# Second product of an expert placed between the halves of the next expert's first product

## The chip, the cores and the metric

The kernel runs on one core of a Trainium2 chip. Times are device microseconds (us) of one execution of the whole program. TensorE (PE in the profile; PEld is its weight load) multiplies, VectorE (DVE) and ScalarE (ACT) work element by element, GpSimd (POOL) builds selections and issues indirect DMAs, SyncE (SP) issues the other DMAs. On-chip memory is SBUF; products gather in PSUM.

## The reference

One layer of a backbone: a token mixer, then a mixture of experts with 32 experts, of which every token goes to 4. The change is in the experts:

```python
def expert_block(args):
    xb, e = args
    hb = xb @ w1[e] + b1[e]
    x_glu = jnp.minimum(hb[:, ::2], SWIGLU_LIMIT)
    x_lin = jnp.clip(hb[:, 1::2], -SWIGLU_LIMIT, SWIGLU_LIMIT)
    act = x_glu * jax.nn.sigmoid(SWIGLU_ALPHA * x_glu) * (x_lin + 1)
    return act @ w2[e] + b2[e]
...
contrib = out[dest].astype(jnp.float32) * sorted_gate[:, None]
return jax.ops.segment_sum(contrib, sorted_tok, num_segments=n_tok).astype(h.dtype)
```

There are 1024 tokens of width 1024. `w1[e]` is 1024 x 2048 and `w2[e]` 1024 x 1024, in float32: 12 MiB of weights for each expert, 384 MiB in all, each read once.

## The kernel before

After the mixer (some 560 us; the routing overlaps the first experts) `experts` (line 1232) runs over 32 places `r`. The experts are sorted by load, and the places alternate a large and a small one: `CAPS[r]` is 122, 122, 126, 122, 132, 120 and so on to 176, 78, 182, 66 token columns.

An expert's weights come as 12 blocks of 1 MiB (`block`, line 1438): blocks 0 to 3 are the first half (1024 columns) of `w1`, 4 to 7 the second half, 8 to 11 are `w2`. They lie in ten buffers `raw`. SP issues the loads in the order of use, each as soon as a buffer is free (`loads`, line 1256). VectorE derives a low part of each block (`lower`, line 1446; buffers `lo`), because a product is made of three float16 or bfloat16 products. Lowering runs `AHEAD` = 4 blocks ahead of TensorE.

TensorE works in 12 units for each expert. A unit (`product`, line 1454) has 48 matmuls and uses two blocks: first-product units are (q, s) with quarter q of 0 to 3 and half s of the inner dimension; the second product has q of 4 and 5 in the order (4,0), (5,0), (4,1), (5,1). In all three parts of an expert the first two of its four blocks are used by s = 0 and the last two by s = 1. When a quarter of the first product is complete, `swiglu` (line 1487) turns it into a quarter of `act` in three stages, one in each of the following units; stages two and three need VectorE after ScalarE. A second-product unit with s = 0 reads quarters 0 and 1 of `act`, one with s = 1 quarters 2 and 3.

The schedule is a hand-written order in the loop at line 1388: `u` counts units, `t = u % 12` is the unit of the expert. In each unit are issued, in this order: the matmuls, the loads that became possible, the second halves of earlier transposes (`rest`), the lowering of block `u + 4`, one stage of each waiting swiglu or output step (`pend`), and then side work: transposes of the rows gathered for the next expert (`turn`, line 1326, from t = 7), transposes of the finished output rows of the expert before (`finish`, line 1343, from t = 1) whose rest scales the rows by their gate and adds them into DRAM by an indirect DMA on POOL (`acc`), the slots' index work for two experts (`batch`, line 1283, t = 5), the selection matrix of a later expert on POOL (`select`, line 1270, t = 0), and the indirect gather of a later expert's rows on POOL (`gather`, line 1321, t = 11). At t = 8 all swiglu stages that are left are issued at once, since the third unit of the second product (t = 10) needs them. Each scatter into `acc` waits on POOL for the landing of the one before. Every engine takes its own instructions in the order in which they were issued.

Of the kernel before, what the change touches and what calls it, by code (L numbers as in the profile page):

```python
# [12 lines left out]
F16 = mybir.dt.float16  # L13
# [11 lines left out]
NE = 32  # L25
# [28 lines left out]
CAPS = [BY_LOAD[q] for q in ORDER]  # L54
# [57 lines left out]
class K:  # L112
# [73 lines left out]
    def mixing(self, p1, up, sm, pm, pt, po):  # L186
# [767 lines left out]

        def channels(ct, U, V):
            pa = bank()
# [275 lines left out]
    def experts(self, routing):  # L1232

        nc, T = self.nc, self.T

        STEPS = [(q, s) for q in range(4) for s in range(2)] + [(4, 0), (5, 0), (4, 1), (5, 1)]
        U = [(r, q, s) for r in range(NE) for q, s in STEPS]
        used = lambda u: [u - u % 12 + 4 * (U[u][1] // 2) + 2 * U[u][2] + i for i in range(2)]  # L1240
        last = {v: u for u in range(len(U)) for v in used(u)}
        raw, low, info, B, X, A, Y, pss = {}, {}, {}, {}, {}, {}, {}, {}
        reg = {}
# [1 line left out]
        freed = set()  # L1245

        def load(u):
            r, b = u // 12, u % 12
            if b == 0:
                reg[r] = nc.sync.value_load(self.eid[0:1, r:r + 1], min_val=0, max_val=NE - 1)  # L1250
                B[r] = self.es_.tile([128, 24], F32, name="bias", bufs=3)
            raw[u] = self.block(reg[r], b // 4, b % 4)
            if b == 0:
                nc.sync.dma_start(B[r], self.biasd[:, bass.ds(reg[r], 1), :].rearrange("p a j -> p (a j)"))

        def loads(spare=0):
# [13 lines left out]
        def select(r, engine=nc.gpsimd, sel=None):  # L1270
            w = width(r)
            if sel is None:
                sel = self.ep.tile([128, NT, CMAX], BF, name="sel", bufs=3)
            if engine is nc.gpsimd:
                for t in range(NT):
                    engine.tensor_scalar(sel[:, t, 0:w], self.places[:, 0:w], self.prk[:, t, r:r + 1], None, op0=OP.is_equal)  # L1276
            else:
                nc.vector.tensor_tensor(sel[:, :, 0:w], self.places[:, None, 0:w].to_broadcast([128, NT, w]), self.prk[:, :, r:r + 1].to_broadcast([128, NT, w]), op=OP.is_equal)
            if CAPS[r] < ROWS[r]:
                engine.memset(sel[:, :, CAPS[r]:ROWS[r]], 0.0)  # L1280
            return sel
# [39 lines left out]
        def gather(r, name="rows"):  # L1321
            for b, (m, idx, gate) in enumerate(info[r]):
                rows[r, b] = self.ep.tile([128, D], F32, name=name, bufs=2)
                nc.gpsimd.indirect_dma_start(out=rows[r, b][0:m, :], out_offset=None, in_=self.Hd, in_offset=bass.IndirectOffsetOnAxis(ap=idx[0:m, :], axis=0))  # L1324

        def turn(r):

            if r >= NE:
                return []
            n = CAPS[r]  # L1330
            X[r] = self.ep.tile([128, 8, 3, n], F16, name="xT", bufs=2)
            out = []
            for b in range((n + 127) // 128):
                m = min(128, n - b * 128)
                parted = [(0, 4), (4, 8)] if m > 64 else [(0, 8)]
                out += [lambda b=b, m=m, ks=ks: self.turn(rows[r, b], X[r], ks, b, m) for ks in parted]
            return out

        def run(q):
            while q:  # L1340
                q.pop(0)()

        def finish(r):

            if r < 0:
                return []
            out = {}

            def step(b, m, idx, gate, h):
                if h == 0:  # L1350
                    out[b] = self.ep.tile([128, D], F32, name="orow", bufs=2)
                ps = self.px.tile([128, 4, 128], F32, name="px")
                for k in range(4):
                    nc.tensor.transpose(ps[0:m, k, :], Y[r][:, 4 * h + k, b * 128:b * 128 + m], self.ident)  # L1354

                def rest():
                    nc.scalar.activation(out[b][0:m, h * 512:(h + 1) * 512], ps[0:m].rearrange("p a n -> p (a n)"), AF.Copy, scale=gate[0:m, :])  # L1357
                    if h:
                        nc.gpsimd.indirect_dma_start(out=self.acc, out_offset=bass.IndirectOffsetOnAxis(ap=idx[0:m, :], axis=0), in_=out[b][0:m, :], in_offset=None, compute_op=OP.add)  # L1359

                return rest

            return [lambda b=b, m=m, idx=idx, gate=gate, h=h: step(b, m, idx, gate, h) for b, (m, idx, gate) in enumerate(info[r]) for h in range(2)]

        sels = {}
# [20 lines left out]

        pend, side, rest = [], [], []
        for u, (r, q, s) in enumerate(U):
            n, t = CAPS[r], u % 12
            bias = lambda j, r=r: B[r][:, j:j + 1]  # L1390
            if t == 0:
                A[r] = self.ep.tile([128, 8, 3, n], F16, name="act", bufs=1)
                side = finish(r - 1)
            if t == 7:
                side = turn(r + 1)
            if t == 8:
                Y[r] = yT
            if not s:
                pss[r, q] = self.ph.tile([128, 2, 512], F32, name="ph")
            ps = pss[r, q]  # L1400
            self.product(ps, [raw[v] for v in used(u)], [low[v] for v in used(u)], q % 2, s, X[r] if q < 4 else A[r], n, q < 4)
            for v in used(u):
                if last[v] == u:
                    del raw[v], low[v]
                    freed.add(v)
            loads()
            run(rest)
            lower(u + AHEAD)

            for st in [stages.pop(0) for stages in pend]:  # L1410
                st()
            if t == 8:
                for stages in pend:
                    run(stages)
            pend = [stages for stages in pend if stages]
            if side and t not in (0, 6):
                rest.append(side.pop(0)())
            if s:
                pend.append(self.swiglu(ps, q, A[r], n, bias) if q < 4 else self.yout(ps, 4 * (q - 4), Y[r], n, bias))
            if r == 2 and t in (3, 5):  # L1420
                next(routing)
            if t == 5 and r % 2 == 0 and r + 2 < NE:
                batch([r + 2, r + 3], [sels[r + 2], sels[r + 3]])
            if r == 0 and t in (2, 3):
                sels[t] = select(t, nc.vector)
            if t == (0 if r else 4) and r + 4 < NE:
                sels[r + 4] = select(r + 4)
            if t == 11:
                assert not side
                if r + 2 < NE:  # L1430
                    gather(r + 2)
        run(rest)
        for stages in pend:
            run(stages)
# [86 lines left out]
    def expert(self, n, e, fetched, bias):  # L1521
        nc = self.nc
        xT, blocks = fetched

        def sums(h, x):

            raw = [self.block(e, h, b) for b in range(4)]
            lo = [self.lower(r) for r in raw]
            for g in range(2):
                ps = self.ph.tile([128, 2, 512], F32, name="ph")  # L1530
                for s in range(2):
                    self.product(ps, raw[2 * s:2 * s + 2], lo[2 * s:2 * s + 2], g, s, x, n, h < 2)
                yield ps

        act = self.ep.tile([128, 8, 3, n], F16, name="act", bufs=1)
        for h in range(2):
            for g, ps in enumerate(sums(h, xT)):
                for st in self.swiglu(ps, 2 * h + g, act, n, bias):
                    st()
        yT = self.ep.tile([128, 8, CMAX], F32, name="yT", bufs=1)  # L1540
        for g, ps in enumerate(sums(2, act)):
            for st in self.yout(ps, 4 * g, yT, n, bias):
                st()
        for b, (m, idx, inf) in enumerate(blocks):
            o = self.ep.tile([128, D], F32, name="orow", bufs=2)
            for g in range(2):
                ps = self.px.tile([128, 4, 128], F32, name="px")
                for k in range(4):
                    nc.tensor.transpose(ps[0:m, k, :], yT[:, 4 * g + k, b * 128:b * 128 + m], self.ident)
                nc.scalar.activation(o[0:m, g * 512:(g + 1) * 512], ps[0:m].rearrange("p a n -> p (a n)"), AF.Copy, scale=inf[0:m, 7:8])  # L1550
            nc.gpsimd.indirect_dma_start(out=self.acc, out_offset=bass.IndirectOffsetOnAxis(ap=idx[0:m, 0:1], axis=0), in_=o[0:m, :], in_offset=None, compute_op=OP.add)
# [71 lines left out]
```

## Time and profile before

| | us |
|---|---|
| median of 3 runs | 1779.34 |
| lowest and highest | 1773.02, 1780.84 |
| the profiled execution | 1778.57 |
| its span | 1776.7 |

Of the span some 560 us are the mixer and the start of the routing, the loop over the experts runs from there to some 1740 us, and the rest is the end of the last outputs and the final norm. In the rows below, a window's "busy" is the time in which an engine had at least one instruction under way; "DMA share" is the mean busy share of the 16 DMA engines, and can pass 1 where packets overlap. "[1.59 <-DMA raw]" behind an instruction says how long its engine was idle before it and what ended that.

### The profile page before, as it was taken

Reading aid. Unit: us, or ns where it says so; the run is one execution under the profiler, and the core shown is the slowest. Engines: PE = TensorE matmul, PEld = TensorE weight load, DVE = VectorE, ACT = ScalarE, POOL = GpSimd, SP = SyncE. Lnnn points to the kernel's source line nnn. Section 1 sums busy time; section 2 is a strip of 40 time slices with the busy share of each in tenths; the row PEclk is TensorE's granted clock in tenths of the full one; section 3 lists DMA queues with packets and bytes.
Section 4 is the critical chain, followed back from the end, with each engine's and each line's share of the span. In section 5 each row is a group of like instructions: output and inputs, shape, how many; then the busy total and the mean of one; then the engine's idle time right before and its main releaser. Section 6 shows DMA issues by size and latency. Waiting matters only on the chain.

```text
span 1776.7 us, 52599 instructions
## 1 busy us (share of the span) xinstructions
PE 1665.5 (94%) x22354; PEld 1456.7 (82%) x22354; DVE 1460.2 (82%) x2350; ACT 641.7 (36%) x1695; POOL 725.0 (41%) x381
## 2 busy tenths in 40 slices
PE   5999999899995999999999999999999999999991
PEld 2455776545665999999999999999999999999891
DVE  4687886856668989998899898898989889898872
ACT  6442213233221334334343333433334343343333
POOL 0000001200005626765577456766577666750101
PEclk9899999999996999999999999999999999999996
DMA  9415521123327999999999999999999999999986
GB/s 340 131 56 162 152 74 38 57 95 111 118 99 293 372 368 363 395 381 383 368 370 390 359 370 380 371 388 371 368 366 364 379 369 366 384 359 374 372 288 214
DMA packets 161199, 513.31 MB, mean 289 GB/s; under 512 B 20896, under 2 KB 21496, under 8 KB 160960
## 3 DMA queue, kind: packets, MB, share of 16 engines
q1 hardware_dynamic: 144256, 467.45, 70.2%
q0 software_dynamic: 10656, 34.14, 7.9%
q10 hardware_dynamic: 6048, 8.31, 1.5%
q8 instruction: 177, 2.90, 0.7%
q14 instruction: 62, 0.51, 0.1%
HBM read 477.71 MB, written 32.13 MB: 287 GB/s over the span
## 4 chain that ended last, share of the span: by engine, by line
PE 48%; DMA 9%; DVE 4%; issue 2%; ACT 0%; POOL 0%; POOLq 0%; SPq 0%; DVEq 0%
PE ph L1468 44%; DMA raw<-in_expert_w_dram 7%; DVE lo L1451 2%; PE px L1354 2%; DMA acc<-orow,idx 1%; PE px L1476 1%; PE px L1295 1%; DVE act L1509 1%; DVE lin L1503 0%; ACT act L1507 0%; DVE xT L1483 0%; DVE raw L1229 0%; DMA raw<-acc 0%; POOL ss L125 0%; DVE lin L1499 0%
## 5 line engine op out<-in xcount | busy, mean ns | idle before, releaser
L1451 DVE CUSTOM_DVE_ANT_0 lo<-raw 128x2048 f16<-128x2048 f32 x384 | 878.9, 2308 | 35.2 <-DMA raw<-in_expert_w_dram 30.7
L1468 PEld LDWEIGHTS <-raw 128*128 128x128 bf16 x12288 | 733.9, 109 | 23.6 <-issue 21.4
L1468 PE MATMUL ph<-xT,raw 128*128 128x108 f16 (+20 forms) x8192 | 512.0, 220 | 2.2 <-issue 1.3
L1276 POOL TENSOR_SCALAR sel<-rows,prk 128x146 bf16<-128x146 f32 (+10 forms) x224 | 502.5, 2257 | 4.0 <-PE px L1295 2.8
L1468 PEld LDWEIGHTS <-lo 128*128 128x128 f16 x6144 | 366.6, 98 | 4.3 <-issue 4.3
L1468 PE MATMUL ph<-act,raw 128*128 128x108 f16 (+20 forms) x4096 | 263.3, 221 | 15.2 <-DVE act L1509 9.3
L1468 PE MATMUL ph<-xT,lo 128*128 128x108 f16 (+20 forms) x4096 | 273.6, 219 | 4.0 <-issue 4.0
L1359 POOL DMA_INDIRECT acc<-orow,idx x46 | 122.5, 2663 | 276.6 <-ACT orow L1357 116.1
L1324 POOL DMA_INDIRECT rows<-Hd,idx x45 | 59.6, 1325 | 228.2 <-PE px L1476 122.9
L266 PE MATMUL mm<-u 128*128 128x512 f32 x512 | 147.8, 424 | 1.5 <-ACT u L528 1.5
L1507 ACT ACTIVATE act<-lin 128x244 f16<-128x244 f32 (+20 forms) x128 | 53.4, 417 | 255.1 <-DVE lin L1503 241.8
L1357 ACT ACTIVATE orow<-px,inf 128x512 f32<-128x512 f32 (+17 forms) x92 | 63.3, 689 | 216.1 <-PE px L1354 215.9
L1468 PE MATMUL ph<-act,lo 128*128 128x108 f16 (+20 forms) x2048 | 139.1, 222 | 0.0
L1517 ACT ACTIVATE yT<-ph,bias,m5s 128x122 f32<-128x122 f32 (+20 forms) x256 | 96.4, 458 | 112.1 <-PE ph L1468 112.1
L266 PE MATMUL mm<-u,h 128*128 128x512 bf16 x512 | 132.3, 392 | 0.6 <-DVE h L530 0.6
L266 PE MATMUL mm<-h,u 128*128 128x512 bf16 x512 | 126.0, 383 | 0.0
L125 POOL TENSOR_TENSOR ss<-ss,mhalf 128x1 f32<-128x1 f32 x26 | 16.2, 623 | 258.6 <-DVE ss L124 227.2
L266 PEld LDWEIGHTS mm<-u 128*128 128x128 f32 x512 | 95.8, 191 | 28.0 <-ACT u L528 4.5
L125 POOL TENSOR_TENSOR v<-v,mhalf 128x8 f32<-128x8 f32 x8 | 14.3, 1784 | 200.0 <-DVE v L124 200.0
L266 PEld LDWEIGHTS <-u 128*128 128x128 bf16 x512 | 49.1, 99 | 56.5 <-issue 3.1
L266 PEld LDWEIGHTS <-h 128*128 128x128 bf16 x512 | 45.6, 99 | 60.4 <-issue 14.1
L1481 ACT ACTIVATE xT<-px 128x512 f16<-128x512 f32 (+17 forms) x78 | 40.1, 514 | 135.8 <-PE px L1476 135.8
(288 smaller groups left out, 1663.8 us busy)
## 6 DMA issues: line engine op xcount, KB each, us to landing
raw<-in_expert_w_dram SPq DMA_DIRECT2D x384, 1024.0 KB
u<-in_mod_w_dram SPq DMA_DIRECT2D x96, 256.0 KB
u<-in_w_in_dram SPq DMA_DIRECT2D x40, 256.0 KB
u<-in_x_dram SPq DMA_DIRECT2D x16, 256.0 KB
u<-in_w_out_dram SPq DMA_DIRECT2D x16, 256.0 KB
u<-in_x_dram ACTq DMA_DIRECT2D x16, 256.0 KB
acc<-u SPq DMA_DIRECT2D x16, 256.0 KB
Hd<-u SPq DMA_DIRECT2D x16, 256.0 KB
```

The costliest lines, as they stand in the source:

```text
L125: nc.gpsimd.tensor_tensor(out, out, self.mhalf[:, 0:out.shape[1]], op=OP.pow)
L266: nc.tensor.matmul(ps, l, r, start=i == 0, stop=i == 3 * n - 1)
L1276: engine.tensor_scalar(sel[:, t, 0:w], self.places[:, 0:w], self.prk[:, t, r:r + 1], None, op0=OP.is_equal)
L1324: nc.gpsimd.indirect_dma_start(out=rows[r, b][0:m, :], out_offset=None, in_=self.Hd, in_offset=bass.IndirectOffsetOnAxis(ap=idx[0:m, :], a ...
L1354: nc.tensor.transpose(ps[0:m, k, :], Y[r][:, 4 * h + k, b * 128:b * 128 + m], self.ident)
L1357: nc.scalar.activation(out[b][0:m, h * 512:(h + 1) * 512], ps[0:m].rearrange("p a n -> p (a n)"), AF.Copy, scale=gate[0:m, :])
L1359: nc.gpsimd.indirect_dma_start(out=self.acc, out_offset=bass.IndirectOffsetOnAxis(ap=idx[0:m, :], axis=0), in_=out[b][0:m, :], in_offset=N ...
L1451: self.nc.vector.tensor_tensor_reduce(flat(lo), flat(raw), flat(raw).bitcast(BF)[:, 1::2], LIFT, 0.0, OP.subtract, OP.max, most)
L1468: nc.tensor.matmul(o, w[k // 2][:, k % 2, c, g, :], x[:, 4 * s + k, i, :], start=not (s or i or g or k), stop=s == 1 and i == 2 and k == 3 ...
L1481: nc.scalar.activation(hi, src, AF.Copy, scale=SX)
L1507: nc.scalar.activation(hi, lin[:, :, 0:n], AF.Copy, scale=SA)
L1517: self.nc.scalar.activation(yT[:, j, 0:n], ps[:, i // 2, i % 2 * n:i % 2 * n + n], AF.Identity, bias=bias(16 + j), scale=self.m5s[:, j:j + 1])
```

## The change

The units of an expert are cut into three groups of four: first half of the first product (0), its second half (1), and the second product (2). `PLAN` orders the groups: (r, 0), (r - 1, 2), (r, 1) for each place r, so the second product of an expert comes between the two halves of the next one's first product. The weight loads follow that order. `act` gets two buffers, since two experts' inner rows are alive at once. The side work is placed anew in a cycle of twelve units that now goes first half (t = 0 to 3), second product of the expert before (4 to 7), second half (8 to 11): `turn` of the next expert from t = 4, `finish` of the expert before from t = 9, `batch` at t = 2, `select` at t = 1, `gather` at t = 11 as before. The flush of the swiglu stages at t = 8 goes; one stands ahead of the last expert's second product, which has nothing in between. At place 0, which has no second product ahead of it, `turn`, `batch` and `select` stand at t = 8.

```diff
-        STEPS = [(q, s) for q in range(4) for s in range(2)] + [(4, 0), (5, 0), (4, 1), (5, 1)]
-        U = [(r, q, s) for r in range(NE) for q, s in STEPS]
-        used = lambda u: [u - u % 12 + 4 * (U[u][1] // 2) + 2 * U[u][2] + i for i in range(2)]
+        PLAN = [g for r in range(NE) for g in ([(r, 0), (r - 1, 2), (r, 1)] if r else [(0, 0), (0, 1)])] + [(NE - 1, 2)]
+
+        STEPS = {0: [(0, 0), (0, 1), (1, 0), (1, 1)], 1: [(2, 0), (2, 1), (3, 0), (3, 1)], 2: [(4, 0), (5, 0), (4, 1), (5, 1)]}
+        U = [(r, q, s) for r, h in PLAN for q, s in STEPS[h]]
+        used = lambda u: [u - u % 4 + 2 * U[u][2] + i for i in range(2)]
...
-            r, b = u // 12, u % 12
-            if b == 0:
+            (r, h), b = PLAN[u // 4], u % 4
+            first = h == b == 0
+            if first:
...
-            raw[u] = self.block(reg[r], b // 4, b % 4)
-            if b == 0:
+            raw[u] = self.block(reg[r], h, b)
+            if first:
...
-            n, t = CAPS[r], u % 12
+            h = PLAN[u // 4][1]
+
+            n, z, t = CAPS[r], r + h // 2, 4 * (0, 2, 1)[h] + u % 4
             bias = lambda j, r=r: B[r][:, j:j + 1]
             if t == 0:
-                A[r] = self.ep.tile([128, 8, 3, n], F16, name="act", bufs=1)
-                side = finish(r - 1)
-            if t == 7:
-                side = turn(r + 1)
-            if t == 8:
+                A[r] = self.ep.tile([128, 8, 3, n], F16, name="act", bufs=2)
+            if t == (4 if z else 8):
+                side += turn(z + 1)
+            if t == 9 and z:
+                assert not side
+                side = finish(z - 1)
+            if t == 4:
                 Y[r] = yT
...
-            if t == 8:
-                for stages in pend:
-                    run(stages)
             pend = [stages for stages in pend if stages]
-            if side and t not in (0, 6):
+            if side:
                 rest.append(side.pop(0)())
...
-            if r == 2 and t in (3, 5):
+            if z == 2 and t in (3, 7):
                 next(routing)
-            if t == 5 and r % 2 == 0 and r + 2 < NE:
-                batch([r + 2, r + 3], [sels[r + 2], sels[r + 3]])
-            if r == 0 and t in (2, 3):
+            if t == (2 if z else 8) and z % 2 == 0 and z + 2 < NE:
+                batch([z + 2, z + 3], [sels[z + 2], sels[z + 3]])
+            if z == 0 and t in (2, 3):
                 sels[t] = select(t, nc.vector)
-            if t == (0 if r else 4) and r + 4 < NE:
-                sels[r + 4] = select(r + 4)
-            if t == 11:
-                assert not side
-                if r + 2 < NE:
-                    gather(r + 2)
+            if t == (1 if z else 8) and z + 4 < NE:
+                sels[z + 4] = select(z + 4)
+            if t == 11 and z + 2 < NE:
+                gather(z + 2)
+            if u == len(U) - 5:
+
+                for stages in pend:
+                    run(stages)
+                pend = []
```

## Rows read from the trace of the kernel before

**Rows 1.** The page, parts 1 and 2: TensorE's busy time; DMA share by slice.
```profile
PE 1665.5 (94%) x22354; PEld 1456.7 (82%) x22354; DVE 1460.2 (82%) x2350; ACT 641.7 (36%) x1695; POOL 725.0 (41%) x381
...
DMA  9415521123327999999999999999999999999986
```

**Rows 2.** Windows: us, busy of PE, PEld, DVE, ACT, POOL; clock; DMA share; GB/s.
```profile
727.00:799.50 72.50, 72.27 (x1283) 71.71 (x1281) 66.94 (x94) 28.27 (x81) 48.46 (x23) 1.00 1.03 385
...
1166.10:1240.00 73.90, 71.88 (x1239) 71.25 (x1235) 67.44 (x92) 28.36 (x80) 50.74 (x23) 1.00 1.03 378
...
1315.50:1389.10 73.60, 73.60 (x1237) 73.30 (x1234) 66.72 (x89) 27.82 (x78) 49.32 (x23) 1.00 1.01 366
...
1537.50:1612.90 75.40, 75.30 (x1240) 74.95 (x1236) 67.12 (x90) 29.88 (x82) 32.32 (x16) 1.00 1.02 369
...
639.76:1719.70 1079.94, 1062.77 (x17909) 1054.57 (x17907) 970.86 (x1311) 413.12 (x1163) 627.73 (x294) 0.99 1.02 371
...
1367.70:1411.10 43.40, 43.40 (x629) 43.36 (x626) 38.37 (x53) 14.02 (x38) 29.24 (x15) 1.00 1.03 378
```

**Rows 3.** Windows of single experts, line 1468 alone: us, PE, PEld; clock, DMA, GB/s.
```profile
817.20:854.50 37.30, 33.34 (x580) 32.46 (x578) 0.95 1.03 375
...
1260.50:1294.90 34.40, 30.76 (x579) 29.94 (x577) 0.95 1.01 372
...
1336.60:1367.70 31.10, 28.85 (x580) 28.35 (x578) 1.00 1.01 364
...
1485.60:1515.60 30.00, 27.68 (x579) 27.11 (x577) 1.00 1.01 372
...
1713.00:1739.00 26.00, 20.80 (x579) 20.43 (x576) 0.93 0.66 199
```

**Rows 4.** The chain of waits (start us, us, what) and one row of VectorE's timeline.
```profile
1269.85 15.00 DMA raw<-in_expert_w_dram
...
1289.03 11.00 PE ph L1468 x164
...
1641.91 12.67 DMA raw<-in_expert_w_dram
...
1284.87 2.29 DVE L1451 CUSTOM_DVE_ANT_0 lo<-raw 128x2048 f16<-128x2048 f32 x1 [1.59 <-DMA raw<-in_expert_w_dram]
```

**Rows 5.** Timeline of TensorE in the first expert.
```profile
588.10 2.00 PE L1468 MATMUL ph<-act,raw 128*128 128x122 f16 x27 [2.62 <-DVE act L1509]
```

**Rows 6.** Two windows of 25 us, columns as in rows 2.
```profile
740.00:765.00 25.00, 25.00 (x452) 24.81 (x450) 24.23 (x25) 10.94 (x30) 20.88 (x9) 1.00 1.03 405
...
1340.00:1365.00 25.00, 25.00 (x485) 24.75 (x483) 22.88 (x31) 11.59 (x34) 14.42 (x8) 1.00 1.01 357
```

**Rows 7.** POOL: one selection; gathers (ns min/median/max) and their landing; scatters.
```profile
1364.24 19.36 POOL L1276 TENSOR_SCALAR sel<-rows,prk 128x170 bf16<-128x170 f32 x8
...
L1324 POOL DMA_INDIRECT rows<-Hd,idx x45: 910/1057/3082, 550.6 to 1658.6; - x45
...
DMA to landing us min/median/max: 7.7/9.3/10.7
...
L1359 POOL DMA_INDIRECT acc<-orow,idx x46: 1422/2721/3648, 610.7 to 1741.7; - x46
```

**Rows 8.** The end: timelines of TensorE and VectorE; the chain's three scatters.
```profile
1727.96 0.55 PE L1468 MATMUL ph<-xT,lo 128*128 128x66 f16 x13 [2.67 <-issue]
...
1737.28 1.15 PE L1468 MATMUL ph<-act,raw 128*128 128x66 f16 x32
...
1738.75 1.85 PE L1354 MATMUL px<-misc,yT 128*70 128x128 f32 x8
...
1730.88 2.29 DVE L1451 CUSTOM_DVE_ANT_0 lo<-raw 128x2048 f16<-128x2048 f32 x1 [1.55 <-SPq L1578]
...
1719.74 10.54 DMA acc<-orow,idx
1731.08 6.75 DMA acc<-orow,idx
1741.68 5.36 DMA acc<-orow,idx
```

More of the change, by code (lines that the diff above doesn't have):

```diff
@@ L1533, in sums @@
                 yield ps
-        act = self.ep.tile([128, 8, 3, n], F16, name="act", bufs=1)
+        act = self.ep.tile([128, 8, 3, n], F16, name="act", bufs=2)
         for h in range(2):
```

## The prediction

> **What bounds the kernel now.** Read the shares first [rows 1]: TensorE is busy 94% of the span, and from the thirteenth slice on the 16 DMA engines stand at 9 tenths nearly throughout. So the expert loop, which fills the span from some 560 to 1740 us, is pressed from two sides, and a share alone does not say which of them ends a stretch. Next the loop cut at pairs of experts (one large, one small, 24 weight loads each) [rows 2]: of twelve such pairs the first takes 72.5 and the last 75.4 us, the DMA share is 1.01 to 1.03 in each, and the rate stays within 366 and 385 GB/s. Where TensorE is busy for the whole pair (1315.5 to 1389.1) the DMA engines are full too. Both are used up at once.
>
> Then single experts [rows 3]. The same 576 matmuls of 108 columns take 31.1 us in one expert (from 1336.6), but 34.4 in another (from 1260.5). The chain of waits shows what the longer one holds [rows 4]: a weight load in flight for 15.00 us, the lowering of that block (2.29 us), swiglu steps of VectorE and ScalarE, and only then TensorE, 1.9 us after the lowering. VectorE takes its instructions in order, and it had stood idle for that load (1.59 us) with the last swiglu of the first product queued behind the lowering. TensorE stands in the third unit of the second product, the first that needs that swiglu. The chain has nine such loads, the last at 1641.91, so the wait is frequent; but it exists because a load is late.
>
> **The change, part by part.** *Waits for the swiglu.* After the change four units of another expert lie between a first product and its second, so its last swiglu has four units more to pass VectorE's queue. What TensorE loses now, from [rows 3]: 31.1 us at 108 columns and 30.0 at 104 make 0.27 us a column, hence some 33.8 at 118 and 20 at 66 columns. Six small experts lie above their line; the first of them (118 columns, 37.3 us) by 3.5, that of 34.4 us by 3.3, the last (66 columns, 26.0 us) by 6, all six together by some 25. With the first expert's wait of 2.62 us [rows 5] that is 27 us. Not all of it is this wait: in the last expert 2.67 us are one pause in mid-product that nothing releases [rows 8].
>
> *What a shorter wait can be worth.* Only as much as the loads allow. The stretch from 639.76 to 1719.70 (all but the first two experts and the last units) moves 371 GB/s in the mean [rows 2], 400.7 MB in 1079.9 us, and the change moves the same bytes. At 378 GB/s, which the pair from 1166.1 reaches, they take 1060 us: 20 us less. At 373.6, the mean of the twelve pairs from 727 to 1612.9, they take 1072: 7 less. The rate sags where few loads are under way: 357 against 405 GB/s in two stretches in which TensorE never rests [rows 6] (gathers and scatters may be in flight for more of the slower one, so not all of that is the sag). Before, twelve fast units follow twelve slow ones; after, four follow four, and buffers come free more evenly. Ends 0 and 20; I take 10, between the mean pair and the good pair.
>
> *Loads in another order.* The 384 loads, their sizes and the ten buffers stay; no SP instruction is added, and SP's 32 bias loads keep their count. *Two act buffers* cost SBUF, no instruction. *The flush* that ran all swiglu stages at the ninth unit goes, and comes once, before the last second product: the same instructions. Nothing on ScalarE or VectorE is added. *Batch and selection* move by three units and one; the slots of `batch` are needed by the gather nine units later. Each of these is 0.
>
> *Turn and gather.* The rows of the next expert are turned from unit 4 on instead of unit 7, four units before they are used, so VectorE's share of it comes earlier, beside a stretch without swiglu. But on POOL the gather now stands right behind the scatter-add of the expert before, both sent at unit 11, and the first turn comes six units later. From the start of unit 11: some 1.2 us to the scatter (an estimate; at the end the last transposes start at 1738.75, eight in place of four, and the scatter 2.9 us later [rows 8]), 2.7 for its issue, 1.1 for the gather's issue, 9.3 to its landing [rows 7]: 14.3 us. The six units last 3.6+4x2.6+3.6 = 17.6 us with experts of 162 and 108 columns, a twelfth of their experts' time each (43.4 and 31.1 us) [rows 2, 3]. It fits with 3.3 us to spare. POOL's selection of 19.4 us [rows 7] starts at unit 1 and ends before unit 11, since ten units last 30 us. Cost 0, with a rival below.
>
> *The end.* The last block is lowered from 1730.88 on and TensorE ends its last product at 1738.8 [rows 8]: 7.9 us. Its order within the last four units is unchanged; a block that is waited for needs 2.3 us of lowering and two units of 1.47 (1737.28 to 1738.75), 5.2 us. Gain 0 to 2.7; I take 2. Against it: the scatters of the last but one expert move. They went out at the second to fifth unit of the last expert; now the first goes at unit 11 and the second in the last four units. Scatters wait for each other's landing (10.54 us, after 0.8 the second with 6.75, then the last with 5.36) [rows 8]. In the trace the third is issued 2.9 us after TensorE's end, when the second had landed. After the change, with units of 1.47 us, the first is issued 6.2 us before the end; at today's landings the third would land 18 us after the end (-6.2+10.5+0.8+6.8+0.8+5.4), against 8.3 now: +9.8. If all three take 5.4 us, because the loads are done, 11.5: +3.2. I take +7. Behind it 29.7 us of final norm stay as they are.
>
> Sum: -10 -2 +7 = **-5 us** on the profiled execution's 1778.57, so 1773.6; the median of the three runs lies 0.8 above that execution, so **1774**.
>
> *A rule that speaks against the change.* The Trainium skill (Perfetto Trace Analysis, Engine Utilization) puts a core's whole memory bandwidth at 358 GB/s. The pairs here move 366 to 385 and one stretch 405 GB/s [rows 2, 6], so the figure is passed, and the measurement decides. By the rule's sense, that a loop at full bandwidth has nothing left to win, the sum would be the third case's below.
>
> **The rivals.** *TensorE alone sets the end.* For it: in whole pairs it never rests [rows 2]. Then the 27 us come back in full, with -2 and +7: -22, 1757. Against it: the DMA share of 1.01 to 1.03. *The transfers are a hard floor.* For it: that share, also in the pairs with waits. Then the loop keeps its length, TensorE waits for blocks where it waited for the swiglu, and only the end is left: +7, 1786. Against it: the sag to 357 GB/s. *The gather comes late.* Its place is the first turn, unit 4; it decides if the gathered rows land later than 17.6 us after unit 11 began, so if POOL is over 3.3 us behind (its selection of 19 us may start late, behind a scatter that waits for the landing of the one before, 10.5 us [rows 7, 8]). TensorE then stands in front of the transposes, and all that follows in its queue with it: the next half product, the other transposes. With 2 us for each of the 14 experts of two blocks that is 28 us, 1774+28 = 1802. *The change does not do what it says*, for example since VectorE waits for the load in any case and the swiglu is late in the same measure: then 1779.
>
> **How the numbers follow.** The forecast (1774, its own ends 1778.6-20-2.7+3.2+0.8 = 1760 and 1778.6+9.8+0.8 = 1789) gets 0.48. TensorE alone 0.18, the hard floor 0.15, the late gather 0.14, no effect 0.05. The range of 8 in 10 reaches from 1760 to 1790: outside lie half of the first rival, most of the late gather, and the tips. A measurement of this kernel tells about 0.5% from no change, that is 8.9 us: faster is below 1770.4, slower above 1788.2. Faster: two fifths of the forecast, 0.19, and 0.18, together 0.37. Slower: a third of the floor, 0.05, and the late gather, 0.14, together 0.19. Between: 0.44.
>
> **What would show it.** In the changed kernel's chain the detours load, lowering, swiglu steps, TensorE should be gone; loads may stand directly before a first product. The pairs' rate should lie nearer to 378 than to 371, and experts of equal width take equal time. After TensorE's last product the three scatters should stand in a row for 11 to 18 us. If TensorE waits for gathered rows at the transposes, the late gather is right. If the DMA share falls well below 1 in the loop while TensorE never rests, my floor was wrong and the gain is larger.

## The result and the profile after

The changed kernel takes **1788.21 us** (median, 1787.21 to 1792.01), the kernel before 1779.34: ratio 1.0067, 95% interval 1.0053 to 1.0081. The forecast was 1774 with a gain of 5; the time is inside the range of 8 in 10, on the wrong side of "before". The profiled execution of after has a span of 1789.2 us against 1776.7, 12.5 more. Line numbers of after are 3 to 7 higher than before: the products stand at 1475, the lowering at 1458, the turn's transposes at 1483, the gather at 1327, the scatter into `acc` at 1362, the selection at 1279, the last swiglu stage at 1514 to 1516.

The page of after, part 1: the engines' busy time, for [rows 1].

```profile
PE 1660.4 (93%) x22309; PEld 1453.9 (81%) x22354; DVE 1463.8 (82%) x2350; ACT 640.1 (36%) x1695; POOL 597.7 (33%) x381
```

TensorE has the same work (1660 us against 1665, some matmuls being missing from either trace), so the 12.5 us are time in which it stood or ran slowly. What it stood for is in the waits. First of **before**, TensorE's waits of 560 to 1760 us (line waited at, releaser; us in total, times, longest):

```profile
PE ph L1468 <- DVE act L1509: 9.3, 19, 2.6
PE ph L1468 <- issue: 6.2, 5, 2.7
PE ph L1468 <- ACT act L1507: 4.5, 6, 0.8
PE px L1187 <- DVE tb L1185: 2.2, 1, 2.2
PE px L1153 <- DVE ecol L1151: 0.9, 1, 0.9
PE ph L1468 <- DVE xT L1483: 0.9, 1, 0.9
```

The same view of **after**:

```profile
PE px L1483 <- DMA rows<-Hd,idx: 19.1, 11, 5.3
PE ph L1475 <- DVE most L1458: 6.2, 6, 2.3
PE px L1153 <- DVE nb L1154: 4.2, 1, 4.2
PE px L1187 <- DVE tb L1185: 3.1, 1, 3.1
PE px L1298 <- DVE sel L1283: 1.5, 1, 1.5
PE ph L1475 <- issue: 1.4, 2, 1.1
PE ph L1475 <- DVE xT L1490: 0.9, 1, 0.9
```

The change did what it says: the two rows for `act`, 13.8 us, are gone completely. In their place stand 19.1 us in eleven waits of the turn's transposes for gathered rows, 6.2 for a lowering, and 8.8 instead of 3.1 in the routing's and the batch's small products. The sums are 24.0 and 36.4 us, 12.4 apart. Of the span's 12.5 us, 9.8 lie before the end of the last product (1738.9 before, 1748.7 after) and 2.7 behind it, so 2.6 of the waits were made good elsewhere; where, is open.

One of the waits, in the order of POOL's and TensorE's work (start, duration, engine, what; the idle time before in brackets):

```profile
1251.52 1.94 POOL L1362 DMA_INDIRECT acc<-orow,idx  x1 [11.38 <-ACT orow L1360]
1253.76 1.52 POOL L1327 DMA_INDIRECT rows<-Hd,idx  x1 [0.30 <-PE ph L1475]
1255.59 2.19 POOL L1327 DMA_INDIRECT rows<-Hd,idx  x1 [0.30 <-issue]
```

TensorE in the same stretch: the start of unit 11, two plain units, the end of the unit at which the turn stands, and the turn:

```profile
1250.33 2.27 PE L1475 MATMUL ph<-xT,raw 128*128 128x150 f16 x32
...
1255.78 1.70 PE L1475 MATMUL ph<-xT,raw 128*128 128x108 f16 x32
...
1258.09 1.70 PE L1475 MATMUL ph<-xT,raw 128*128 128x108 f16 x32
...
1264.79 1.20 PE L1475 MATMUL ph<-act,lo 128*128 128x150 f16 x16
1267.09 0.63 PE L1483 MATMUL px<-misc,rows 128*128 128x128 f32 x4 [1.09 <-DMA rows<-Hd,idx]
```

POOL had idled 11.38 us in front of the scatter, which waits for ScalarE's scaling of the finished rows; the gather, next in POOL's order, could not start before it. TensorE, done with the products of that unit at 1266.0, stood until 1267.09, 13.3 us after the gather's start. The view of the gather's line gives the time from the start of a gather's issue to the landing of its rows, for the 16 gathers whose landing the trace holds (compare 7.7, 9.3 and 10.7 in [rows 7], which are of seven):

```profile
DMA to landing us min/median/max: 8.8/12.6/15.3
```

The dearest wait stands in the chain that ended last (start, us, what):

```profile
1634.47 15.31 DMA rows<-Hd,idx
...
1651.00 5.34 PE ph L1475 x48
```

The 5 us behind it in a window (stretch, us, busy time of PE, PEld, DVE, ACT, POOL, then clock, DMA share, GB/s):

```profile
1650.00:1655.00 5.00, 5.00 (x37) 4.93 (x38) 2.85 (x4) 1.08 (x2) 0.00 (x0) 0.56 1.02 388
```

After standing 5.3 us TensorE has a granted clock of 0.56 in the mean of these 5 us, most of them at the lower of its two levels, 1.2 GHz, and one unit of 48 matmuls takes 5.34 us.

The end, POOL's three last scatters, for [rows 8]:

```profile
1741.37 2.00 POOL L1362 DMA_INDIRECT acc<-orow,idx  x1 [28.54 <-ACT orow L1360]
1749.04 1.45 POOL L1362 DMA_INDIRECT acc<-orow,idx  x1 [5.67 <-ACT yT L1524]
1754.59 1.47 POOL L1362 DMA_INDIRECT acc<-orow,idx  x1 [4.10 <-DMA fin<-in_final_norm_w_dram]
```

The chain in that stretch:

```profile
1744.25 4.43 PE ph L1475 x144
...
1754.59 5.05 DMA acc<-orow,idx
```

The last product ends at 1748.7 and the third scatter has landed at 1759.6, 11.0 us later, where it was 8.3. The scatters stand in a row, as forecast.

### The profile page after: what moved, and what is told of

It is laid out like the page before. It is cut to its first block, busy times and chain, and to the rows that moved or that the text cites. A ratio compares the mean times of both kernels' runs of the same rounds, so it can differ in the third digit from the quotient of the medians.

```text
span 1789.2 us, 52602 instructions
## 1 busy us (share of the span) xinstructions
PE 1660.4 (93%) x22309; PEld 1453.9 (81%) x22354; DVE 1463.8 (82%) x2350; ACT 640.1 (36%) x1695; POOL 597.7 (33%) x381
## 5 line engine op out<-in xcount | busy, mean ns | idle before, releaser
L1279 POOL TENSOR_SCALAR sel<-rows,prk 128x146 bf16<-128x146 f32 (+10 forms) x224 | 383.8, 2177 | 2.2 <-PE px L1298 1.6
L1362 POOL DMA_INDIRECT acc<-orow,idx x46 | 100.9, 2194 | 608.4 <-ACT orow L1360 424.3
L266 PE MATMUL mm<-u,h 128*128 128x512 bf16 x488 | 127.7, 391 | 2.5 <-DVE h L530 0.9
L1327 POOL DMA_INDIRECT rows<-Hd,idx x45 | 78.9, 1754 | 38.3 <-DVE inf L1313 20.8
L1503 ACT ACTIVATE lin<-ph,bias 128x122 f32<-128x122 f32 (+20 forms) x256 | 78.4, 358 | 32.6 <-PE ph L1475 25.4
```

The source lines that it names most:

```text
L266: nc.tensor.matmul(ps, l, r, start=i == 0, stop=i == 3 * n - 1)
L1503: nc.scalar.activation(lin[:, c, 0:n], ps[:, c, n:2 * n], AF.Identity, scale=1.0 / SX, bias=bias(8 + 2 * q + c))
```

## The experiments

Theory L: the gather is too late, because it is issued behind the scatter; nothing else is wrong with the change. Rivals: the loss lies in the routing and batch waits of the first experts; in POOL's selection, which holds up its queue; in the place of the turn; and for the size of the gain: the transfers are the floor. Each ratio below is to executions of the kernel before that were taken beside the run; their medians are 1777.6 to 1778.7 us.

**e1, the gather three units earlier in the order.**

```
-            if t == 11 and z + 2 < NE:
+            if t == 8 and z + 2 < NE:
                 gather(z + 2)
```

> The changed kernel with one edit: the gather of a later expert's rows is issued at unit 8 of the cycle in place of unit 11, so on POOL it stands behind the selection and ahead of the scatter-add. Theory L (the changed kernel lost its gain at the first turn, where TensorE waits 17.2 us in ten places for gathered rows from 700 us on, and runs at half clock for 3.4 us after the longer ones): these waits are gone and the time falls by 17 to 25 us, from 1788 to 1763 to 1771, below the kernel before. Theory F (the transfers are the floor, and the wait for the rows only stands where a wait for weights would stand): TensorE waits for lowered blocks instead, the time stays at 1783 to 1788.

Measured: **1765.87 us** (1761.25 to 1768.08), ratio to before 0.9927 (0.9903 to 0.9951), 22 us below the changed kernel. TensorE's waits of 560 to 1760 us:

```profile
PE ph L1475 <- DVE most L1458: 7.6, 7, 2.1
PE px L1153 <- DVE nb L1154: 4.0, 1, 4.0
PE px L1187 <- DVE tb L1185: 3.0, 1, 3.0
PE px L1298 <- DVE sel L1283: 1.9, 1, 1.9
PE ph L1475 <- issue: 0.5, 1, 0.5
```

No wait for rows is left, and none for `act`. This is theory L, and a kernel that beats both. The 7.6 us of waits for lowered blocks, 6.2 in the changed kernel, are new against the kernel before.

**e2, e1 and the batch of the third expert three units later,** out of the way of the routing.

```
-            if t == (2 if z else 8) and z % 2 == 0 and z + 2 < NE:
+            if t == ((5 if z == 2 else 2) if z else 8) and z % 2 == 0 and z + 2 < NE:
```

> As e1_gather_early, and in the third place (z = 2) alone the index work of two experts (batch) is issued at unit 5 in place of unit 2, so that its twelve small VectorE instructions no longer stand ahead of the routing steps that TensorE waits for at units 3 and 7. Theory R (the routing waits of 4.2 and 3.1 us, against 0.9 and 2.2 in the kernel before, and the half clock behind them, cost the early loop some 5 us): 4 to 7 us less than e1_gather_early. Rival: that time is given back while the later loop is held by its loads: no difference above 2 us.

Measured: 1763.33 us (1759.5 to 1767.36), 0.9914 (0.9881 to 0.9947). The two waits at the routing are 2.8 and 4.0 us instead of 4.0 and 3.0. The difference from e1 lies within the interval: neither shown nor excluded. But the two waits are 6.8 us together, where e1 has 7.0, so moving the batch did not take them away.

**e10, the gather one unit earlier,** just ahead of the scatter.

```
-            if t == 11 and z + 2 < NE:
+            if t == 10 and z + 2 < NE:
                 gather(z + 2)
```

> The changed kernel with the gather one unit earlier (t == 10 for 11), which puts it ahead of the scatter of the same turn on POOL's queue and in the transfers, as before the change; the turn stays at t == 4. Theory L split in two. By order (the gather lands late because it is started behind the scatter's issue, 1.4 to 3.7 us, and its rows come behind the scatter's transfer, 12.6 us median to landing against 9.3 before): start one unit of about 2.6 us and 2.5 us of issue earlier, and landing in 9 to 10 us, together some 8 us earlier than in the changed kernel, where the longest waits are 5.3 us: no wait for rows is left, 1764 to 1770, as with the gather three units earlier. By distance alone (order is of no matter, the landing stays at 12 to 13 us): 2.6 us earlier, half of the 17 us of waits stays, 1772 to 1782.

Measured: **1765.06 us** (1762.35 to 1768.56), 0.9918 (0.9886 to 0.995): the whole gain of e1 for one unit, as expected by order. POOL's rows for the same expert as above, and for the small one after it:

```profile
1241.48 1.94 POOL L1327 DMA_INDIRECT rows<-Hd,idx  x1 [0.67 <-PE ph L1475]
...
1245.81 2.84 POOL L1362 DMA_INDIRECT acc<-orow,idx  x1 [0.30 <-issue]
...
1263.41 1.06 POOL L1327 DMA_INDIRECT rows<-Hd,idx  x1 [0.19 <-issue]
1278.49 3.21 POOL L1362 DMA_INDIRECT acc<-orow,idx  x1 [14.02 <-ACT orow L1360]
```

The first gather starts 4.3 us ahead of the turn's scatter, where it stood 2.2 behind it; the last one 15.1 ahead, though its call is one unit earlier. A call in the loop is a place in POOL's queue and no time: freed from the scatter, a gather goes as soon as its indices and buffers are there. The landing takes 9.7 us in the median, not 12.6, though not of the same gathers: the traces hold 27 landings here and 16 there. Experts of more than 128 columns have two gathers. For the first of the two, in the loop, the median is 12.8 us in the changed kernel (11.3 to 15.3) and 10.5 in e1 (9.1 to 12.8), where it also stands ahead of the scatter. No wait of TensorE for rows is left in e10.

**e7, the changed kernel with the selections made by VectorE.**

```
-                sels[z + 4] = select(z + 4)
+                sels[z + 4] = select(z + 4, nc.vector)
```

> The changed kernel with that same move of the selection to VectorE, nothing else: gather at t == 11, turn at t == 4. Theory L (the gather is late because it is called too late and lands 12 to 13 us after its start, behind the scatter's transfer; a long selection matters for the stall at the sixteenth and seldom elsewhere): about a third of the 17 us of waits for rows goes, VectorE's additional work takes some back: 1780 to 1790. Theory P (the selection on POOL is the main cause of the late gathers in the changed kernel too): waits for rows below 4 us and a time of 1764 to 1772, like e1.

Measured: 1787.22 us (1782.42 to 1789.37), 1.0046 (1.0028 to 1.0065). TensorE's waits for rows:

```profile
PE px L1483 <- DMA rows<-Hd,idx: 19.6, 11, 5.0
```

With no selection on POOL at all the waits for rows are what they were. The selection is not what makes the gather late in the changed kernel. One of its eleven waits, 3.3 us at 1191, does have a selection ahead of the scatter: it ended at 1175.0, 3 us after unit 11 had begun.

**e8, e1 with that move.**

```
-                sels[z + 4] = select(z + 4)
+                sels[z + 4] = select(z + 4, nc.vector)
-            if t == 11 and z + 2 < NE:
+            if t == 8 and z + 2 < NE:
```

> e1 (gather at t == 8) with the selection moved to VectorE. In e1 no wait for gathered rows is left, so the move has nothing to give there; it prices the 34 us of work that it puts on VectorE. If VectorE has room (busy 0.91 of e1's loop, idle 64 us in it waiting for loads): within 3 us of e1, 1763 to 1769. If VectorE's order is what limits e1: 1775 to 1800.

Measured: 1771.36 us (1766.63 to 1774.66), 0.9958 (0.9945 to 0.9971): 5.5 us above e1, between the two bounds. So VectorE has room for most of the 34 us that the move puts on it, and not for all.

**e3, the turn one unit later,** which should have given the gather the time it lacks.

```
-            if t == (4 if z else 8):
+            if t == (5 if z else 8):
                 side += turn(z + 1)
```

> The changed kernel with one other edit: the gather stays at unit 11, but the first turn stands at unit 5 in place of 4, one unit of 2.2 to 3.8 us later. Theory L: each wait for gathered rows shrinks by one unit, ten waits of 17.2 us in all to two or three of together 3 to 6 us, time 1770 to 1778. Theory F: no difference, 1785 to 1790.

Measured: **1917.58 us** (1912.21 to 1945.92), 1.0767 (1.0726 to 1.0808). The expectation failed by 140 us, and the waits for rows are 160.8 us in eleven (its profile is of an execution of 1945.92 us, so its waits add up to more than the medians differ by; the profile of e5, below, shows the same at 1894.58 us). POOL at the first of them:

```profile
783.02 45.02 POOL L1279 TENSOR_SCALAR sel<-rows,prk 128x138 bf16<-128x138 f32 x8
828.25 1.68 POOL L1362 DMA_INDIRECT acc<-orow,idx  x1 [0.20 <-issue]
830.24 1.02 POOL L1327 DMA_INDIRECT rows<-Hd,idx  x1 [0.30 <-issue]
...
832.51 4.88 POOL L1279 TENSOR_SCALAR sel<-rows,prk 128x138 bf16<-128x138 f32 x8
```

The same eight instructions take 45.02 us the first time and 4.88 the second. The two stretches in windows (columns as above):

```profile
796.00:828.00 32.00, 27.87 (x484) 27.51 (x481) 31.58 (x41) 12.07 (x36) 32.00 (x3) 1.00 1.02 401
832.50:837.40 4.90, 0.00 (x0) 0.00 (x0) 0.00 (x0) 0.00 (x0) 4.88 (x8) 0.50 1.02 303
```

In the long one VectorE is busy 31.58 of 32.00 us, in the short one not at all. So POOL is shut out while VectorE works; scatter and gather queue behind; TensorE stands for the rows; VectorE runs dry; POOL catches up in 5 us; and the game begins anew two experts on.

**e5, the turn later and the gather earlier.**

```
-            if t == (4 if z else 8):
+            if t == (5 if z else 8):
-            if t == 11 and z + 2 < NE:
+            if t == 8 and z + 2 < NE:
```

> The changed kernel with the turn one unit later (t == 5), as in e3, and the gather three units earlier (t == 8), as in e1. Theory Q (the loss in e3 comes only from gathers queued on POOL behind a long selection and a scatter; the later turn by itself costs nothing): the gather at t == 8 has its rows in SBUF long before, so the time is that of e1, 1762 to 1770. Rival T (the turn at t == 5 is itself what costs in e3, for example because its transposes and copies then run beside more of the second product, or because the row buffers come free later and hold the next gather back): most of e3's 140 us stay, over 1850; a few of them, 1775 to 1800, if only the row buffers do it.

Measured: 1897.61 us (1885.74 to 1902.24), 1.0668 (1.0622 to 1.0714), 113.1 us of waits for rows. Theory Q falls: a gather three units earlier is still behind the selection in POOL's queue, and that takes 43 us here too.

**e6, e3 with the selections made by VectorE.**

```
-            if t == (4 if z else 8):
+            if t == (5 if z else 8):
-                sels[z + 4] = select(z + 4)
+                sels[z + 4] = select(z + 4, nc.vector)
```

> e3 (turn at t == 5, gather at t == 11) with the selection of every expert from the fifth on made by VectorE in one instruction (1.21 us each in the records of e1, 28 of them, so 34 us more on VectorE, which is busy 984 of 1080 us in e1's loop), and no longer by eight instructions on POOL. Theory P (POOL's selection, drawn out to 43 us while VectorE is busy without a gap, is what holds scatter and gather back in e3): the waits of TensorE for gathered rows, 160.8 us in e3, fall below 15 us and the time to 1765 to 1795, the upper end if VectorE's 34 us show. Rival: the gathers are late for another reason (the scatter alone, or TensorE's own lag): the waits stay over 80 us and the time over 1850.

Measured: 1823.71 and 1871.54 us; the profile is of the second. There the waits are 90.4 us, and not below the 15 expected. What is left on POOL is shut out as well:

```profile
1396.77 19.37 POOL L1362 DMA_INDIRECT acc<-orow,idx  x1 [22.81 <-ACT orow L1360]
```

The issue of one scatter, 1.4 to 3.7 us in the changed kernel, takes 19.37 us, in a stretch in which VectorE is busy 17.85 of 17.90.

**e9, e3 with short pauses for POOL.**

```
             run(rest)
+            if z and t in (7, 8, 9, 10):
+                pad = self.es_.tile([128, 128], F32, name="pad", bufs=1)
+                for _ in range(2):
+                    nc.vector.memset(pad, 0.0)
             lower(u + AHEAD)
```

> e3 (turn at t == 5, gather at t == 11) with two short writes of a constant by VectorE (128 x 128, about 0.15 us each by the nearest rows, small operations of 0.15 to 0.3 us) ahead of the lowering in the units t = 7 to 10 of each turn: 31 x 4 x 2 = 248 instructions, some 40 us more work for VectorE. Theory P (VectorE's lowerings and its other operations on two operands in SBUF, one behind the other without a gap, keep POOL's instructions from starting; in the records those went through beside VectorE's operations on PSUM and beside small ones): the four places let one or two selecting instructions through each, the selections of 43 us shorten to below 30 us, and of TensorE's 160.8 us of waits for gathered rows more than half goes: 1800 to 1860 in spite of the additional work. Rival (only an idle VectorE lets POOL through; or the late rows have another cause): no selection is shorter, and the time is 1910 to 1960.

Measured: **1771.35 us** (1767.5 to 1775.13), 0.9962 (0.9945 to 0.998): 146 us less than e3 for 41.2 us more work on VectorE. One of the selections, which take up to 45 us in e3, with the pauses at its end:

```profile
1152.30 17.71 POOL L1279 TENSOR_SCALAR sel<-rows,prk 128x156 bf16<-128x156 f32 x8
...
1166.93 0.42 DVE L1418 MEMSET pad<- 128x128 f32 x2
...
1169.49 0.42 DVE L1418 MEMSET pad<- 128x128 f32 x2
```

And TensorE's waits for gathered rows (the turn is line 1487 here):

```profile
PE px L1487 <- DMA rows<-Hd,idx: 1.5, 1, 1.5
```

The seventh selecting instruction ends at 1167.6, beside the first of these pauses, the eighth at 1170.0, beside the second. So the cause of e3's loss is that VectorE shuts POOL out, and not the later turn by itself (theory T of e5).

**e11, the same pauses in the changed kernel,** the turn at t == 4 as there.

```
             run(rest)
+            if z and t in (7, 8, 9, 10):
...
             lower(u + AHEAD)
```

> The changed kernel as it is (turn at t == 4, gather at t == 11) with the short writes of e9 (41.2 us of VectorE in e9's records) in the units t = 7 to 10. It asks how much of the changed kernel's 19 us of waits for rows comes from POOL being shut out by VectorE, which e3 and e9 showed with the turn one unit later. Theory O (order: the gather stands behind the scatter, which waits for the products' last transposes, and lands 12 to 13 us after its start; e10): the waits shrink only where a selection was long (the sixteenth) and mostly stay, 10 to 17 us; 1780 to 1790. Theory P (shut-out is the main cause here too): waits for rows below 4 us, 1765 to 1773.

Measured: 1784.44 us (1780.13 to 1798.77), 1.005 (1.0023 to 1.0076), and 18.4 us of waits for rows in fourteen, none over 3.0. Theory O: where the turn stands at unit 4 the pauses take the peaks off, and the order keeps the rest. By the two ratios the pauses are worth some 3 us, but the intervals overlap, so a gain is not shown.

**b4 and e4, half of each weight load left out,** in the kernel before and in e1, with each lowering made in two halves from the loaded part; the products use the loaded half twice.

```
-        self.nc.sync.dma_start(raw, src[:, 2 * b:2 * b + 2, c0:c0 + 1024])
+        self.nc.sync.dma_start(raw[:, 0, :], src[:, 2 * b, c0:c0 + 1024])
```

> The kernel before with half of each weight load left out: each block's load brings its first 512 KB alone, and product and lowering use that half twice, so TensorE, VectorE and ScalarE keep their work (the lowering is two instructions of half the length). It shows what the loop takes when the transfers cannot hold it. If loads that come late are what stands behind the waits of the kernel before, the waits for the last swiglu go and the time falls by some 25 us to 1750 to 1757. If the order of VectorE's queue alone makes them, whatever the loads do, the time stays within 1770 to 1780.

> e1 (gather at t == 8) with only half of each weight load, and each lowering split into two on the half that is loaded, as in b4 on the kernel before; half of the products' operands are thereby wrong. b4 showed 1792, with 23.8 us of TensorE waiting for act and 49 us more of VectorE. Theory A (the change's gain lies in the waits for act, which VectorE's queue makes whether or not transfers are full): those 24 us are gone here, and the time is 1762 to 1775. Theory D (the gain in e1 lies in the transfers running with fewer pauses, 371 GB/s rising): with the transfers out of the way there is no gain, 1788 to 1796. A third course, from e3 and e5: VectorE never waits for a load here, so that POOL's instructions could be shut out and the rows be late again: waits for gathered rows of over 30 us, over 1800.

Measured: b4 1792.32 us (one execution), e4 **1763.45** (1763.14 to 1763.72; 0.9913, 0.9886 to 0.9941 to the whole kernel before). b4's loop in a window (columns as above):

```profile
640.00:1700.00 1060.00, 1034.34 (x17479) 1024.14 (x17477) 990.92 (x1970) 403.44 (x1135) 393.90 (x294) 0.99 0.66 200
```

Its first two waits of TensorE, for `act`:

```profile
PE ph L1469 <- ACT act L1508: 15.0, 20, 1.0
PE ph L1469 <- DVE act L1510: 14.9, 29, 3.1
```

e4's loop in the same window:

```profile
640.00:1700.00 1060.00, 1052.73 (x17911) 1046.77 (x17912) 1024.74 (x2003) 410.06 (x1163) 399.93 (x293) 1.00 0.68 204
```

With transfers at 200 GB/s the waits for `act` are not smaller but larger, 29.9 us against 13.8. They need no late load; the order of VectorE's queue is enough for them. How much of the 13.8 us in the kernel before late loads add is not shown, since b4's VectorE also has 39 us more work in this window. In the new order e4, with the same half loads and the same additional work, has none of these waits and is 29 us faster, theory A. And with half the transfers it is only 2.4 us faster than e1, and 1.6 faster than e10, which was measured beside it: once the gather is in time, full transfers cost little (VectorE's additional work in e4 may hide a part). The third course did not come: POOL's longest selecting instruction takes 3.3 us in e4, although VectorE is busy 97% of its loop. Beside lowerings of half the length POOL got through.

## Why the prediction was wrong

**The failed step is "It fits with 3.3 us to spare".** The rival "the gather comes late" is what happened, at the place that it names. The condition that it sets did not decide: it asks for rows that land over 17.6 us after unit 11 began, with POOL 3.3 us behind. In the example unit 11 began at 1250.33, the scatter started 1.2 us later, as in the sum, and the gather 3.4 us after unit 11's start, where the sum had 3.9. POOL was not behind. TensorE stood all the same, for rows that came 16.8 us after unit 11 began.

Two terms of the sum were mis-sized. The time until the turn: the six units took 15.7 us in place of 17.6. A twelfth of an expert's time, 2.6 us at 108 columns, holds the expert's side work too, while a plain unit runs at 2.31 us (1255.78 to 1258.09); four of those make 1.2 of the 1.9 us, and the two outer units have 150 columns here and 162 in the sum. The landing: 9.3 us was the median of seven gathers in other places. The first of two gathers in the new place, with a scatter 2 to 4 us ahead, takes 12.8 in the median, and 13.3 in the example; ahead of the scatter it takes 10.5 (e1), so standing behind the scatter makes some 2 us of it. A landing is counted from the start of the gather's issue, so the sum's 1.1 us for the issue were in the 9.3 already, which hid a part of the error. Counted from the scatter's start, the turn was due after 14.5 us, where the sum had 16.4, and the rows came after 15.6, where it had 13.1. Either error alone would have left 0.8 or 1.4 us to spare; both together made it 1.1 late.

The other waits are of the same kind. In the eleven the turn was due 14.9 to 16.2 us after unit 11 began and the rows landed after 16.1 to 20.0, in seven of them within the 17.6 that the rival sets. That the selection "ends before unit 11" failed in one, the wait at 1191. What would have helped is in the queue: e10 shows that one place there moves the gather's start, against the scatter, by 6.5 us and more, and that with it the waits for rows are gone. Before the change the gather waited mostly for the turn's transposes to free its buffers and for its indices, not for a scatter.

**The rival's price** was 2 us for each of 14; measured were 1.7 in the mean of eleven, 19.1 in all, but up to 5.3 us late in the loop, and some microseconds of half clock after the long ones. In all it costs 22 us (1788.2 against 1765.9 in e1) where the rival had 28, and it starts from 8 us less than the forecast's 1774: hence 1788 and not 1802. The mechanism, a gather that lands behind its turn, was right; its chance of 0.14 was too small.

**The gain in the loop, -10, is real, and its reason was wrong.** With the gather in time the waits for `act` are gone. In their place e1 has 7.6 us of waits for lowered blocks and more at the routing, so the sums of waits are 24.0 before and 17.0 in e1, 7.0 us apart. From the start of the first product to the end of the last the profiles of e1 and e10 take 12.7 and 14.5 us less than that of before (1165.5 and 1163.7 against 1178.2); what makes up the rest is open. "It exists because a load is late" and "only as much as the loads allow" are not borne out: b4 has the waits without a late load, and e4, with half the transfers, gains only some 2 us more than e1 and e10. The rival "TensorE alone sets the end", 1757 at 0.18, comes nearer, and e1, e2 and e10 at 1763 to 1766 lie between it and the forecast. But its 27 us were not all such waits: in the view of before the waits for `act` are 13.8 us, 6.2 more are pauses that nothing releases, and 4.0 lie elsewhere. The floor of the transfers, 1786, is refuted: e1 and e10 move the same bytes in a shorter loop. A DMA share of 1.01 to 1.03 meant that the engines had something in flight, at rates of 357 as well as 405 GB/s [rows 6], not that they could not be faster. One reading is off by a slice: the DMA row [rows 1] stands at 7 tenths in the thirteenth and at 9 from the fourteenth on; nothing rests on it.

**"Each of these is 0"** (batch and selection) was wrong by 5.7 us: 3.1 before, 8.8 after in the three rows of small products. The batch at unit 2 of the third expert puts its small VectorE operations in front of the routing's. That this is the reason is not shown, and e2 speaks against it: it moved the batch, and the two waits at the routing stayed.

**The end, -2 and +7,** came out in kind for its second term alone. The last block is lowered from 1739.65 on, and the last product ends 9.0 us later, where it was 7.9 before, so the gain of 2 did not come. The scatters stand in a row; the last two take some 5 us each, so 11.0 us from product to landing, near the lower bound of 11.5, and +2.7 in place of +7. In e1 it is 13.7 us (1720.8 to 1734.5), nearer to the +7.

**What stays open.** Why the turn one unit later shuts POOL out at 783 us, where the changed kernel's POOL got through in the same expert, isn't settled: VectorE is nearly as busy there (17.18 of 17.90 us against 31.58 of 32.00). Some of the lowerings there took 2.4 us instead of 2.27; in e3 none from 800 to 828 us did.

## What to carry to other kernels

Take the time until a DMA's rows are used from plain units, and its landing from DMAs with the same neighbours; a few microseconds to spare that come out of means are not a margin. A call on an engine's queue is a place in an order, so price a moved DMA by what stands ahead of it there and what that waits for, and see what one place further ahead would give; a gather behind a scatter starts when the scatter's data are ready. When VectorE has little slack, look at POOL's longest instruction, not only at its share: one instruction of 31 us in front of a DMA, as in e3, became a stall.

## What the runs showed of the hardware

POOL's work beside a busy VectorE was not expected. Eight selecting instructions took 4.88 us beside an idle VectorE, 9 to 26 us in the changed kernel's loop and up to 45 us in e3 beside lowerings back to back; the issue of a scatter 1.4 to 3.7 us in the changed kernel and up to 19.6 in e6. The rows of e3 in that stretch, with the end of a transposed row's step (line 1490), show where one instruction got through:

```profile
796.36 0.63 DVE L1490 SCALAR_TENSOR_TENSOR xT<-px,xT 128x472 f16<-128x472 f32 x1
...
796.92 2.27 DVE L1458 CUSTOM_DVE_ANT_0 lo<-raw 128x2048 f16<-128x2048 f32 x1
...
802.24 2.28 DVE L1458 CUSTOM_DVE_ANT_0 lo<-raw 128x2048 f16<-128x2048 f32 x1
```

Of the last three selecting instructions one ended at 796.9, behind the step on line 1490, which reads PSUM and one operand in SBUF; the next at 800.0, behind the same step; the last only when VectorE stopped, 28 us later, past eleven lowerings and the small steps between them. Each lowering reads two operands from SBUF (the block as float32 and its upper halves). The Trainium skill (SBUF — State Buffer, Who interferes with whom) says that a VectorE instruction with two SBUF inputs contends with a GpSimd instruction that reads SBUF, and (the same page, Summary: rules for kernel authors) that the second of the two to issue is blocked until the first finishes. The trace agrees on who blocks whom: 31 us for one selecting instruction here, 0.6 beside the idle VectorE. The trace adds that the blocked one need not come next: it lost to eleven lowerings, and in e9 one came through beside each of the two pairs of writes shown, of 0.17 us a write, which read no operand. In e4, with lowerings of half the length, no selecting instruction took over 3.3 us; why, no run shows.
